# The end of a mixture of experts in a two-block network: expert 13's output two units earlier, a deeper weight stream, paired V groups, and another order of block 2's first steps

## The chip, the cores and the metric

The kernel runs on one core of a Trainium2 chip. The metric is the device time of one execution in microseconds (us), as the median of several runs. Before the change it is 2907.27 us, the median of three (2904.99 to 2908.48).

## The reference

The network works on 512 tokens of width 1024. Block 1 has two layers, each with one wide input product, differential attention, a gated convolution, attention to a memory, gates, an output product, a layer norm, and a mixture of 16 experts of which each token takes two, with a second layer norm. Block 2 begins with an RMS norm and one wide product, whose columns feed a recurrent branch (RWKV7), a state-space branch (S5) and gates; a convolutional feed-forward part ends it. Cut to what the change touches:

```python
for l in range(DEPTH):                       # block 1, two layers
    proj = x @ w_in[l]
    q, k, v, cb, cc, cu, qm, gates = jnp.split(proj, ...)
    ...
    x = layer_norm(DEEPNORM_ALPHA * x + mix, ln1_g[l], ln1_b[l])
    f = grouped_moe(x.reshape(B * S, D), w_router, router_bias,
                    w_exp_gate[l], w_exp_up[l], w_exp_down[l]).reshape(B, S, D)
    x = layer_norm(DEEPNORM_ALPHA * x + f, ln2_g[l], ln2_b[l])

def expert_block(args):                      # inside grouped_moe
    xblk, e = args
    h = jax.nn.silu(xblk @ w_gate[e]) * (xblk @ w_up[e])
    return h @ w_down[e]

h = rms_norm(x, norm_mix_pre[l])             # block 2
proj = h @ w_in[l]
gates = jax.nn.sigmoid(proj[..., N_RWKV_COLS + S5_WIDTH:] + b_gate[l])
```

## The kernel before, in words

Each product in 32-bit floats is made of three products of split numbers: high by high, high by low and low by high part. The weights come in units of 512 rows by 512 columns, 1.05 MB. A unit is loaded by SyncE's queue into a buffer (`wraw`, L100), ScalarE writes its high half (`whi`, L109) and VectorE its low half (`wlo`, L110), and TensorE makes 12 products of it for each tile of 128 tokens (L180). Raw units, halves and most other large tiles share one pool of 19 buffers. The program is written out in order: on every engine the instructions run in the order in which the Python emits them, and an engine whose next instruction waits runs nothing behind it.

`run_group` works through a group of units. At each unit it calls `ensure(split_to, load_to)`, which emits the splits up to `deep` units ahead of the current one and the loads `ahead` units further. Groups of order "t" go token tile by token tile, with a step `pre(t)` ahead of each; a group of order "h" goes over two halves of 256 tokens. `late` puts one of the three products of each step last. `tick()` advances side work such as the attention by one step.

`plan_moe` lists the experts: gate (two units, a and b), up (two), and one expert behind them the output product `down` (two units, x and y). I write g15a for a unit of expert 15's gate. The outputs of experts 0 to 13 go to a buffer in memory (`ye`, then `ybuf`); those of 14 and 15 stay on the chip as a high and a low half (`yh` on ScalarE, L1084, and `yl` on VectorE, L1085). The order at the end is

```
g14 u14 d13x d13y | last | g15a g15b u15a u15b d14x d14y d15x d15y | first group of the next stage
```

`last` sets `ahead, deep` to 1, 2 (in the mixture they are 7 and 3), calls `overflow`, which loads a count into a register and tests it in an If (L1147, L1149), and issues eight indirect transfers on GpSimd's queue (L1105). Each gathers 128 rows of `ybuf` and adds them to a tile of the residual, `xres`: two for each of the four token tiles.

`Combine` holds the steps behind the experts, each for one token tile: p (products that add experts 14 and 15 out of `yh` and `yl`, L1230), a (the sum on VectorE, L1237), s (statistics), b or c (the layer norm), and for block 2 r (the inverse root), h (the RMS norm, L1271), t (transposes, L335) and f (the low half of the transposed tile). They are listed in strings. In layer 1 the first group behind is half 0 of the V columns, in order "t", with one string for each tile. In block 2 it is `gate(0)`, in order "h": the first string serves tokens 0 to 255 and the second the rest. `rw_consts` writes constants of the recurrent branch and loads some, ahead of `gate(0)`.

Of the kernel before, what the change touches and what calls it, by code (L numbers as in the profile page):

```python
# [11 lines left out]
F32 = mybir.dt.float32  # L12
# [9 lines left out]
P = 128  # L22
D = 1024
T = 512
# [5 lines left out]
NE = 16  # L30
# [27 lines left out]
class Group:  # L58
# [7 lines left out]
    def __init__(self, units, tiles, operands, evac, free=512, before=None, order="k", pre=None,  # L66
                 lead=0, late=False):
        self.units, self.tiles, self.operands, self.evac, self.free, self.before = units, tiles, operands, evac, free, before
        self.order, self.pre, self.lead, self.last, self.late = order, pre, lead, False, late


@with_exitstack
def tile_kernel(ctx: ExitStack, tc: tile.TileContext, A, out):
# [87 lines left out]
    def run_group(g):  # L161
# [4 lines left out]

        def part(ui, t, cols=None):
            u = g.units[ui]
            if t not in psum:
                psum[t] = pb.tile([P, 512], F32, name="acc", tag="acc")  # L170
            trips = [g.operands(ui, kc, t, u) for kc in range(u.nk)]
            seq = [(kc, n) for kc in range(u.nk) for n in range(len(trips[kc]))]
            if g.late:
                seq.sort(key=lambda i: (i[1] == 2, i))
            for i, (kc, n) in enumerate(seq):
                l, r = trips[kc][n]
                if cols is not None:
                    r = r[:, cols]
                o = psum[t][:l.shape[-1], cols if cols is not None else slice(0, g.free)]
                nc.tensor.matmul(o, l, r, start=(ui == 0 and i == 0), stop=(ui == nu - 1 and i == len(seq) - 1))  # L180
                if state["fine"] and (kc, n) == (1, 2):
                    tick()

        if g.order == "k":
            for ui, u in enumerate(g.units):
                if g.last and ui == nu - 1:
                    ensure(i0 + nu, i0 + nu)
                else:
                    ensure(i0 + ui + state["deep"], i0 + ui + state["deep"] + state["ahead"],
                           step=STEP if g.tiles == 4 and state["deep"] == 2 else None)  # L190
                for t in range(g.tiles):
                    part(ui, t)
                    flush(1)
                    if ui == nu - 1:
                        g.evac(t, psum[t])
                    tick()
                u.raw = u.hi = u.lo = None
            return
        ensure(i0 + nu, i0 + nu + state["ahead"])
        halves = g.order == "h"  # L200
        n = 2 if halves else g.tiles
        for m in range(-g.lead, n):
            if g.pre and m + g.lead < n:
                g.pre(m + g.lead)
            if m < 0:
                continue
            if m == n - 1:
                ensure(i0 + nu + 1, i0 + nu + 1 + state["ahead"])
            for t in range(g.tiles) if halves else [m]:
# [6 lines left out]
                if m or not halves:  # L216
                    g.evac(t, psum[t])
        for u in g.units:
            u.raw = u.hi = u.lo = None
# [382 lines left out]
    def plan_block1(l):  # L602
# [6 lines left out]
        def cols(n):  # L609
            return column(w, l, ld, D, n)  # L610
# [9 lines left out]
        comb = Combine(0)  # L620

        def pre(t):
            if l == 0:
# [7 lines left out]
            if t == NT - 1:  # L631
                for n in ("x", "ln", "cm", "idx", "gs", "selT", "yh", "yl", "cnt", "dst", "orow"):
                    S.pop(n)
        pl.append(tok(cols(IN1["v"]), x, lambda t, p: ev_v(t, p, 0), before=mk((("v", 0), "vt")), order="t", pre=pre,
                      lead=1 - l, late=l > 0))

# [13 lines left out]
        for half in range(2):  # L650
            c = half * 512
            pl.append(tok(cols(IN1["q"] + c), x, rope_evac("q", half), before=mk((("q", half), "qT"))))
            pl.append(tok(cols(IN1["k"] + c), x, rope_evac("k", half), before=mk((("k", half), "kT"))))
            if half:
                pl.append(tok(cols(IN1["v"] + c), x, lambda t, p: ev_v(t, p, 1), before=mk((("v", half), "vt"))))
# [389 lines left out]
    def plan_moe(l):  # L1045
# [52 lines left out]
        def last():  # L1098

            finish(S.pop("route"))  # L1100
            state["ahead"], state["deep"] = 1, 2
            overflow(l)
# [6 lines left out]
        for e in range(NE):  # L1109
# [10 lines left out]
            def nxt(e=e):  # L1120
# [4 lines left out]
                if 0 < e <= NT:  # L1125
                    z = S["x"][(e - 1) // 2][:, (e - 1) % 2, :]
                    nc.scalar.activation(z, z, AF.Copy, scale=float(ALPHA))
                if e == NE - 2:
                    load_ln2(l)
# [3 lines left out]
            if e == 0:  # L1133
                S["moe0", l] = us[0]
            if e == NE - 1:
                pl.append(last)
            pl.append(one(us, lambda e=e: S["xeT"][e], ev_g, before=nxt))
            pl.append(one(eweight("w_exp_up", e, D, 512, 0), lambda e=e: S["xeT"][e], ev_u))
            if e:
                pl += down(e - 1)  # L1140
# [844 lines left out]
    def plan_block2():  # L1985
# [31 lines left out]
        def pre(m):  # L2017
            if m == 0:
                S["xT"] = new_feat("hT")
                S["pre"] = gain("norm_mix_pre_2")  # L2020
                comb.run("p0 p1 p2 p3 a0 s0 a1 b0 s1 r0 h0 t0 b1 f0 r1 a2 h1 t1 s2 f1 b2")
            else:
# [13 lines left out]
        def start0():  # L2036
            bv()

            def chain():
# [3 lines left out]
                yield from rwkv(1)  # L2043
            gens["r"] = spawn(chain())
        def gate(i):
            def ev(t, p):
# [3 lines left out]
                nc.gpsimd.dma_start(gdram[:, n, :], g)  # L2050
            return feat(cols(2304 + i * 512), x, ev, **(dict(order="h", pre=pre, before=rw_consts, late=True) if i == 0 else {}))

# [24 lines left out]

        pl.append(gate(0))
        pl.append(tok(cols(1792), x, ev_u, before=bu, sel=lambda t: slice(t, T, 4)))
        pl.append(start_s5)  # L2080
# [310 lines left out]
```

## Time and profile before

| | |
|---|---|
| median of three runs | 2907.27 us |
| profiled execution | 2902.47 us, its span 2900.5 us |
| mean granted clock of TensorE | 0.969 |
| TensorE busy | 2683.6 us (93%) |
| TensorE weight loads | 2164.9 us (75%) |
| VectorE, ScalarE busy | 1836.5 us (63%), 1314.9 us (45%) |
| GpSimd busy | 390.5 us (13%) |
| HBM over the span | 159 GB/s |

The times in the traces count from the start of the span. PE is TensorE, DVE VectorE, ACT ScalarE, POOL GpSimd and SP SyncE. In a timeline each row has the start, the duration and the instruction, and in brackets the idle time before it with what ended it. The mixture of layer 0 ends near 1050 us and that of layer 1 near 2010 us; these are the two places that the change touches.

### The profile page before, as it was taken

The page shows a single profiled execution, that of the slowest core. Times are in us where ns is not written, and L with a number is a line of the kernel's source. Part 1 is how long each engine was busy: PE and PEld are TensorE (multiplying, and loading weights), DVE is VectorE, ACT ScalarE, POOL GpSimd, SP SyncE. Part 2 cuts the span into 40 slices and gives each one's busy share as a digit, 9 for nine tenths or more (in the row PEclk, how much of TensorE's full clock was granted, in tenths as well). Part 3 has the DMA queues.
Part 4 walks back from the last instruction along what each step waited for, and adds up shares of the span by engine and source line. Part 5 has one row for each costly group of instructions (what it writes and reads, how often), then busy time and mean ns, then how long its engine had stood idle before and what let it go on. Part 6 is the DMA issues. An engine that isn't in the chain of part 4 may idle for free. (4 is left out here: it accounts for less than half of the span.)

```text
span 2900.5 us, 37504 instructions
## 1 busy us (share of the span) xinstructions
PE 2683.6 (93%) x14828; PEld 2164.9 (75%) x14828; DVE 1836.5 (63%) x2947; ACT 1314.9 (45%) x1935; POOL 390.5 (13%) x521
## 2 busy tenths in 40 slices
PE   8889999999899989999999979997978978999998
PEld 6677777887687768777788758875866756788887
DVE  4756555446799974565544579998478475655552
ACT  4334444332687743343533258875233542333441
POOL 2744200001100030000000110003221010000000
PEclk9999999999999999999999989998999989999999
DMA  5222413252999972112132489998321223323231
GB/s 192 88 81 84 166 44 98 92 174 93 370 402 409 366 216 73 59 59 73 59 102 102 148 307 391 409 377 253 124 95 59 70 77 132 117 93 102 73 131 44
DMA packets 223142, 464.25 MB, mean 160 GB/s; under 512 B 9849, under 2 KB 37681, under 8 KB 222448
## 3 DMA queue, kind: packets, MB, share of 16 engines
q1 hardware_dynamic: 194832, 359.69, 35.5%
q0 software_dynamic: 28128, 102.11, 10.0%
q8 instruction: 118, 1.93, 0.3%
q14 instruction: 64, 0.52, 0.1%
HBM read 419.29 MB, written 42.47 MB: 159 GB/s over the span
## 5 line engine op out<-in xcount | busy, mean ns | idle before, releaser
L110 DVE TENSOR_TENSOR wlo<-wraw,whi 128x1024 fp32r<-128x1024 f32 (+1 forms) x473 | 806.8, 1734 | 395.7 <-ACT whi L109 386.8
L109 ACT ACTIVATE whi<-wraw 128x1024 fp32r<-128x1024 f32 (+1 forms) x473 | 671.1, 1454 | 103.3 <-PE acc L180 38.5
L180 PE MATMUL acc<-whi,xeT 128*128 128x512 f32 x1024 | 329.5, 403 | 5.4 <-ACT whi L109 4.3
L180 PE MATMUL acc<-xTh,whi 128*128 128x512 f32 x640 | 257.5, 402 | 0.0
L180 PE MATMUL acc<-xTh,wlo 128*128 128x512 f32 x640 | 251.0, 392 | 1.6 <-DVE wlo L110 1.6
L180 PE MATMUL acc<-xTl,whi 128*128 128x512 f32 x640 | 250.2, 391 | 0.0
L180 PEld LDWEIGHTS acc<-whi,xeT 128*128 128x128 f32 x1024 | 190.8, 192 | 45.1 <-ACT whi L109 6.3
L180 PE MATMUL acc<-wlo,xeT 128*128 128x512 f32 x512 | 203.5, 398 | 6.8 <-DVE wlo L110 6.7
L180 PE MATMUL acc<-whi,xTh 128*128 128x512 f32 x384 | 163.1, 425 | 2.1 <-ACT xTh L338 2.1
L180 PE MATMUL acc<-whi,hT 128*128 128x512 f32 x512 | 162.5, 399 | 0.0
L180 PE MATMUL acc<-wlo,xTh 128*128 128x512 f32 x384 | 153.1, 399 | 0.0
L180 PE MATMUL acc<-whi,xTl 128*128 128x512 f32 x384 | 148.8, 398 | 1.7 <-DVE xTl L343 1.7
L475 ACT ACTIVATE pr<-sc,mx 128x128 f32<-128x128 f32 (+3 forms) x128 | 66.3, 523 | 182.8 <-DVE mx L473 168.4
L180 PE MATMUL acc<-h2Tl,whi 128*128 128x512 f32 (+1 forms) x384 | 144.1, 375 | 2.7 <-DVE h2Tl L343 2.7
L180 PE MATMUL acc<-h2Th,whi 128*128 128x512 f32 (+1 forms) x384 | 143.9, 375 | 2.3 <-ACT h2Th L338 2.3
L180 PE MATMUL acc<-h2Th,wlo 128*128 128x512 f32 (+1 forms) x384 | 143.7, 374 | 0.0
L180 PEld LDWEIGHTS acc<-xTh,wlo 128*128 128x128 f32 x640 | 120.5, 188 | 28.2 <-DVE wlo L110 2.0
L180 PEld LDWEIGHTS acc<-xTl,whi 128*128 128x128 f32 x640 | 120.9, 189 | 22.9
L180 PEld LDWEIGHTS acc<-xTh,whi 128*128 128x128 f32 x640 | 120.7, 189 | 23.0
L180 PEld LDWEIGHTS acc<-wlo,xeT 128*128 128x128 f32 x512 | 98.0, 191 | 31.8 <-DVE wlo L110 10.1
L278 POOL TENSOR_TENSOR ss<-ss,mhalf 128x1 f32<-128x1 f32 x64 | 35.2, 550 | 601.3 <-DVE ss L512 567.9
L180 PE MATMUL acc<-hTh,whi 128*128 128x512 f32 (+1 forms) x272 | 108.4, 405 | 0.2 <-ACT hTh L338 0.2
(689 smaller groups left out, 5619.2 us busy)
## 6 DMA issues: line engine op xcount, KB each, us to landing
wraw<-in_w_in SPq DMA_DIRECT2D x76, 1024.0 KB, 5.3
wraw<-in_w_exp_down SPq DMA_DIRECT2D x63, 1024.0 KB, 9.3
wraw<-in_w_exp_gate SPq DMA_DIRECT2D x62, 1024.0 KB, 8.9
wraw<-in_w_exp_up SPq DMA_DIRECT2D x60, 1024.0 KB, 11.6
wraw<-in_ffn_w_up SPq DMA_DIRECT2D x44, 512.0 KB, 4.6
ybuf<-ye POOLq DMA_DIRECT2D x28, 512.0 KB, 6.8
wraw<-in_w_out SPq DMA_DIRECT2D x12, 1024.0 KB, 5.1
wraw<-in_ffn_w_down SPq DMA_DIRECT2D x10, 1024.0 KB, 5.0
```

The lines of the kernel that those rows point to most:

```text
L109: nc.scalar.activation(u.hi[:, c], u.raw[:, c], AF.Copy)
L110: nc.vector.tensor_tensor(u.lo[:, c], u.raw[:, c], u.hi[:, c], op=ALU.subtract)
L180: nc.tensor.matmul(o, l, r, start=(ui == 0 and i == 0), stop=(ui == nu - 1 and i == len(seq) - 1))
L278: nc.gpsimd.tensor_tensor(o, x, mhalf.to_broadcast(list(x.shape)), op=ALU.pow)
L475: nc.scalar.activation(pr[:, c, :n], sc[c][:, :n], AF.Exp, bias=mx[:, c:c + 1], scale=0.125, accum_out=sm[:, c:c + 1])
```

## The change

The change has four parts.

- The order at the end of both mixtures. The output of expert 13 and `last` come two units earlier, ahead of expert 14's up product. The layer norm's weights are loaded one expert earlier.
- The weight stream. `last` sets `ahead, deep` to 2, 3 instead of 1, 2. The first group of the next stage sets them to 1, 2.
- Layer 1's V columns. The two halves are paired: a group may have a second one in `also`, whose products follow tile by tile. The later group of half 1 goes. The splits of the second half's two units are emitted behind the first `pre`.
- Block 2's start. The first string of steps has another order, another of the three products is put last in `gate(0)` (the one with the low half of the tokens instead of the one with the low half of the weights), and `rw_consts` moves from ahead of `gate(0)` to behind it.

```diff
--- before.py
+++ after.py
@@ -67,6 +67,7 @@
                  lead=0, late=False):
         self.units, self.tiles, self.operands, self.evac, self.free, self.before = units, tiles, operands, evac, free, before
         self.order, self.pre, self.lead, self.last, self.late = order, pre, lead, False, late
+        self.also = None
 
 
 @with_exitstack
@@ -164,14 +165,14 @@
         psum, nu = {}, len(g.units)
         i0 = units.index(g.units[0])
 
-        def part(ui, t, cols=None):
+        def part(ui, t, cols=None, g=g, psum=psum):
             u = g.units[ui]
             if t not in psum:
                 psum[t] = pb.tile([P, 512], F32, name="acc", tag="acc")
             trips = [g.operands(ui, kc, t, u) for kc in range(u.nk)]
             seq = [(kc, n) for kc in range(u.nk) for n in range(len(trips[kc]))]
             if g.late:
-                seq.sort(key=lambda i: (i[1] == 2, i))
+                seq.sort(key=lambda i: (i[1] == g.late, i))
             for i, (kc, n) in enumerate(seq):
                 l, r = trips[kc][n]
                 if cols is not None:
@@ -196,6 +197,7 @@
                     tick()
                 u.raw = u.hi = u.lo = None
             return
+        nall = nu + (len(g.also.units) if g.also else 0)
         ensure(i0 + nu, i0 + nu + state["ahead"])
         halves = g.order == "h"
         n = 2 if halves else g.tiles
@@ -204,8 +206,10 @@
                 g.pre(m + g.lead)
             if m < 0:
                 continue
+            if m == 0 and g.also:
+                ensure(i0 + nall, i0 + nall + state["ahead"])
             if m == n - 1:
-                ensure(i0 + nu + 1, i0 + nu + 1 + state["ahead"])
+                ensure(i0 + nall + 1, i0 + nall + 1 + state["ahead"])
             for t in range(g.tiles) if halves else [m]:
                 for ui in range(nu):
                     part(ui, t, slice(m * 256, m * 256 + 256) if halves else None)
@@ -215,7 +219,13 @@
                     tick()
                 if m or not halves:
                     g.evac(t, psum[t])
-        for u in g.units:
+                if g.also:
+                    p2 = {}
+                    for ui in range(len(g.also.units)):
+                        part(ui, t, None, g.also, p2)
+                        tick()
+                    g.also.evac(t, p2[t])
+        for u in g.units + (g.also.units if g.also else []):
             u.raw = u.hi = u.lo = None
 
     def run(plan):
@@ -619,6 +629,11 @@
             nc.scalar.activation(S["v", half][:, t, :], p, AF.Copy)
         comb = Combine(0)
 
+        def first_v():
+            state["ahead"], state["deep"] = 1, 2
+            for half in range(2):
+                S["v", half] = slot([P, 4, T], F32, "vt")
+
         def pre(t):
             if l == 0:
                 to_feat(S["x"][t // 2][:, t % 2, :], S["xT"], t)
@@ -631,8 +646,14 @@
             if t == NT - 1:
                 for n in ("x", "ln", "cm", "idx", "gs", "selT", "yh", "yl", "cnt", "dst", "orow"):
                     S.pop(n)
-        pl.append(tok(cols(IN1["v"]), x, lambda t, p: ev_v(t, p, 0), before=mk((("v", 0), "vt")), order="t", pre=pre,
-                      lead=1 - l, late=l > 0))
+        if l == 0:
+            pl.append(tok(cols(IN1["v"]), x, lambda t, p: ev_v(t, p, 0), before=mk((("v", 0), "vt")), order="t", pre=pre,
+                          lead=1))
+        else:
+            gs_ = [tok(cols(IN1["v"] + h * 512), x, lambda t, p, h=h: ev_v(t, p, h), order="t", pre=pre, late=2)
+                   for h in range(2)]
+            gs_[0].also, gs_[0].before = gs_[1], first_v
+            pl.append(gs_[0])
 
         def ev_qm(t, p):
             nc.scalar.activation(S["qm"][:, t, :], p, AF.Copy)
@@ -651,7 +672,7 @@
             c = half * 512
             pl.append(tok(cols(IN1["q"] + c), x, rope_evac("q", half), before=mk((("q", half), "qT"))))
             pl.append(tok(cols(IN1["k"] + c), x, rope_evac("k", half), before=mk((("k", half), "kT"))))
-            if half:
+            if half and l == 0:
                 pl.append(tok(cols(IN1["v"] + c), x, lambda t, p: ev_v(t, p, 1), before=mk((("v", half), "vt"))))
 
             def start(half=half):
@@ -1098,7 +1119,7 @@
         def last():
 
             finish(S.pop("route"))
-            state["ahead"], state["deep"] = 1, 2
+            state["ahead"], state["deep"] = 2, 3
             overflow(l)
             for j in range(2):
                 for t in range(NT):
@@ -1125,18 +1146,19 @@
                 if 0 < e <= NT:
                     z = S["x"][(e - 1) // 2][:, (e - 1) % 2, :]
                     nc.scalar.activation(z, z, AF.Copy, scale=float(ALPHA))
-                if e == NE - 2:
+                if e == NE - 3:
                     load_ln2(l)
                 if e + 1 < NE:
                     spawn(expert_in(l, e + 1))
             us = eweight("w_exp_gate", e, D, 512, 0)
             if e == 0:
                 S["moe0", l] = us[0]
-            if e == NE - 1:
+            pl.append(one(us, lambda e=e: S["xeT"][e], ev_g, before=nxt))
+            if e == NE - 2:
+                pl += down(e - 1)
                 pl.append(last)
-            pl.append(one(us, lambda e=e: S["xeT"][e], ev_g, before=nxt))
             pl.append(one(eweight("w_exp_up", e, D, 512, 0), lambda e=e: S["xeT"][e], ev_u))
-            if e:
+            if e and e != NE - 2:
                 pl += down(e - 1)
         pl += down(NE - 1)
         pl.append(drain)
@@ -2018,7 +2040,7 @@
             if m == 0:
                 S["xT"] = new_feat("hT")
                 S["pre"] = gain("norm_mix_pre_2")
-                comb.run("p0 p1 p2 p3 a0 s0 a1 b0 s1 r0 h0 t0 b1 f0 r1 a2 h1 t1 s2 f1 b2")
+                comb.run("p0 p1 p2 p3 a0 s0 a1 s1 b0 b1 r0 a2 r1 h0 t0 h1 t1 f0 f1 s2 b2")
             else:
                 comb.run("a3 r2 s3 h2 t2 b3 f2 r3 h3 t3 f3")
                 for n in ("x", "ln", "cm", "idx", "gs", "selT", "yh", "yl", "cnt", "dst", "orow", "pre"):
@@ -2042,13 +2064,16 @@
                     yield
                 yield from rwkv(1)
             gens["r"] = spawn(chain())
+        def first_g():
+            state["ahead"], state["deep"] = 1, 2
+
         def gate(i):
             def ev(t, p):
                 n = i * 4 + t
                 g = w2k([P, T], F32, "sgt")
                 nc.scalar.activation(g, p, AF.Sigmoid, bias=PV["b_gate_2"][:, n:n + 1])
                 nc.gpsimd.dma_start(gdram[:, n, :], g)
-            return feat(cols(2304 + i * 512), x, ev, **(dict(order="h", pre=pre, before=rw_consts, late=True) if i == 0 else {}))
+            return feat(cols(2304 + i * 512), x, ev, **(dict(order="h", pre=pre, before=first_g, late=1) if i == 0 else {}))
 
         def bu():
             S["s5u"] = slot([P, 16, 4, 32], F32, "s5u")
@@ -2076,6 +2101,7 @@
             s5_end()
 
         pl.append(gate(0))
+        pl.append(rw_consts)
         pl.append(tok(cols(1792), x, ev_u, before=bu, sel=lambda t: slice(t, T, 4)))
         pl.append(start_s5)
         pl.append(feat(cols(1536, 256), x, ev_wag, tiles=2, before=b0))
```

## Rows read from the trace of the kernel before

**Rows 1.** Windows: PE, PEld, DVE, ACT, POOL busy us; PEclk, DMA share, GB/s.

```profile
1014.00:1024.00 10.00, 9.61 (x44) 7.40 (x43) 8.70 (x6) 7.03 (x6) 0.54 (x1) 1.00 1.05 407
1028.00:1032.00 4.00, 2.41 (x11) 1.62 (x10) 3.93 (x2) 3.63 (x3) 3.60 (x1) 1.00 0.08 30
1038.00:1050.00 12.00, 9.28 (x38) 6.66 (x38) 8.86 (x6) 8.18 (x7) 8.41 (x4) 1.00 1.06 252
1061.91:1090.45 28.54, 26.61 (x122) 21.32 (x120) 20.93 (x30) 7.23 (x11) 3.55 (x7) 0.95 0.37 133
2050.00:2075.00 25.00, 25.00 (x144) 25.00 (x143) 5.86 (x5) 7.04 (x10) 5.49 (x11) 0.91 0.59 209
```

**Rows 2.** Waits of PE, 1950 to 2060: us in total, times, longest.

```profile
PE acc L180 <- DVE wlo L110: 3.2, 2, 1.6
```

**Rows 3.** Timeline of DVE, second end: start, us, instruction, idle before.

```profile
2003.32 0.74 DVE L1085 SCALAR_TENSOR_TENSOR yl<-acc,gs,yh 128x512 fp32r<-128x512 f32 x1
2004.22 0.86 DVE L1577 MEMSET rwc<- 128x960 f32 x1
...
2007.47 2.28 DVE L110 TENSOR_TENSOR wlo<-wraw,whi 128x2048 fp32r<-128x2048 f32 x1
2009.68 1.28 DVE L1237 TENSOR_TENSOR xres<-xres,yp 128x512 f32<-128x512 f32 x2
2010.87 1.28 DVE L352 BATCH_NORM_STATS2 lnst<-xres 128x6 f32<-128x512 f32 x2
...
2013.71 1.28 DVE L362 SCALAR_TENSOR_TENSOR xres<-xres,lnmv,lnp 128x1024 f32<-128x1024 f32 x1
...
2019.27 1.28 DVE L1271 SCALAR_TENSOR_TENSOR hpre<-xres,rms,gain 128x1024 f32<-128x1024 f32 x1 [1.21 <-POOL rms L278]
```

**Rows 4.** Timeline of PE, second end.

```profile
2027.04 1.94 PE L335 MATMUL tp<-ident,hpre 128*128 128x128 f32 x8 [4.46 <-DVE hpre L1271]
2028.82 0.58 PE L180 MATMUL acc<-hTh,whi 128*128 128x256 f32 x1
```

**Rows 5.** Timeline of POOL, second end, first and last of eight transfers.

```profile
1982.34 1.63 POOL L1105 DMA_INDIRECT xres<-ybuf,dst  x1 [6.30 <-DMA ybuf<-ye]
...
2000.91 1.55 POOL L1105 DMA_INDIRECT xres<-ybuf,dst  x1 [0.69 <-DMA xres<-ybuf,dst]
```

**Rows 6.** Tile view of xres, the last transfer alone (2000.91).

```profile
DMA to landing us min/median/max: 13.4/13.4/13.4
```

**Rows 7.** Timeline of POOL, first end, first and last of eight.

```profile
1028.29 3.60 POOL L1105 DMA_INDIRECT xres<-ybuf,dst  x1 [7.16 <-DMA ybuf<-ye]
...
1050.49 3.37 POOL L1105 DMA_INDIRECT xres<-ybuf,dst  x1 [0.56 <-DMA xres<-ybuf,dst]
```

**Rows 8.** Timeline of DVE, first end, a0.

```profile
1053.63 1.28 DVE L1237 TENSOR_TENSOR xres<-xres,yp 128x512 f32<-128x512 f32 x2 [1.18 <-DMA xres<-ybuf,dst]
```

**Rows 9.** Tile view of wraw: n0, n1, n2; n1 of the first end.

```profile
L100 SPq DMA_DIRECT2D wraw<-in_w_in x1: 554/554/554, 1970.1 to 1970.1; - x1
...
DMA to landing us min/median/max: 13.2/13.2/13.2
...
L100 SPq DMA_DIRECT2D wraw<-in_w_in x1: 383/383/383, 1987.9 to 1987.9; - x1
...
DMA to landing us min/median/max: 15.8/15.8/15.8
...
L100 SPq DMA_DIRECT2D wraw<-in_w_in x1: 368/368/368, 1990.8 to 1990.8; - x1
...
DMA to landing us min/median/max: 24.2/24.2/24.2
...
L100 SPq DMA_DIRECT2D wraw<-in_w_in x1: 377/377/377, 1033.0 to 1033.0; - x1
...
DMA to landing us min/median/max: 15.2/15.2/15.2
```

**Rows 10.** Timeline of ACT, second end, whi of n1.

```profile
2003.79 1.91 ACT L109 ACTIVATE whi<-wraw 128x2048 fp32r<-128x2048 f32 x1 [1.65 <-DMA wraw<-in_w_in]
```

## The prediction

> **What bounds the kernel now.** I read the share of each engine by stage first, then the waits of TensorE, then the engines' timelines around the two ends of the mixture of experts, then the loads there. Inside the mixture TensorE never stops and the DMA rings are full at 407 GB/s: 44 products in 10 us, so 0.227 us each, and a unit of 1.05 MB (12 products, 2.73 us of TensorE) needs 2.6 us of DMA [rows 1]. So nothing is to be had there. What can be had lies at the two stage ends, which I call the first (layer 0 into layer 1, near 1050 us) and the second (layer 1 into block 2, near 2010 us). There `last` puts eight indirect transfers on the queues, and the rings fall to 252 GB/s at a full busy share while they run [rows 1]. TensorE waits twice for a low half near each end, 3.2 us in all [rows 2]. After the last expert it stands still until VectorE has normalised the first token tiles: at the second end VectorE writes yl (2003.32), the constants of block 2 (2004.22 to 2007.47), the low half of unit n1 (2.28 us), and only then a0, at 2009.68; the first product of block 2 is at 2028.82 [rows 3, 4]. What precedes a0 on VectorE and ScalarE is therefore the path; I call the next stage's first four units n0 to n3.
>
> **The change, part by part.**
>
> **Order at the end.** Expert 13's output (`ye`) comes two units, 2 x 2.73 = 5.5 us, earlier, with the wait at the If behind it some 6 us. The indirect transfers start at 1982.34 and 2000.91 (first and last) and the last lands 13.4 us after its issue, at 2014.3 [rows 5, 6]; moved by 6 they end near 2008.3. At the first end they start at 1028.29 and 1050.49 [rows 7]; with the same 13.4 us the end goes from 1063.9 to 1057.9. That alone is a gain only where a0 waits for them: 1.18 us at the first end [rows 8], none at the second [rows 3].
>
> **What the loads lose by it.** The If makes SP wait until the loads that it has issued have landed: n0, issued at 1970.1, lands 13.2 us later at 1983.3, and the next load, n1, goes out only at 1987.9 [rows 9]. Before, the nine units ahead of d13y reach through d15y and n0. With u14 moved behind `last`, nine ahead reach only d15x. So d15y and n0 change sides: they are issued behind the If, as n1 is. d15x is two loads earlier in the stream, so it lands 2 x 2.6 earlier, at 1978.1, and d15y goes out then, n0 and n1 some 3 us apart behind it, as buffers are freed by the units of expert 15.
>
> Beside the indirect transfers loads crawl. n1 takes 15.8 us, n2 lands at 1990.8 + 24.2 = 2015.0, 11.3 us behind n1: 2.1 MB in 27.1 us, 77 GB/s, where 407 is the rate alone [rows 1, 9]. The first end agrees, 15.2 us for n1 [rows 9]. Three loads now stand where the first of the row stood. d15y: at best it passes before the indirect transfers have filled the rings (6 us, an estimate: twice the 2.6 us of the rate alone and a start), lands 1984; at worst as n1 did, 1993.9. n0 11.3 us behind: 1995.3 to 2005.2. n1 2006.6, or, as the indirect transfers are over at 2008.3 and the rest goes at full rate, 2010.2. I take the middle, 2008.4. At the first end everything stands 954.05 us earlier (1982.34 against 1028.29), so d15y goes out near 1024. There the rings stood nearly empty, share 0.08, for 4 us around the first transfer [rows 1], which favours the near bound: n1 at 1024 + 5 + 2 x 11.3 = 1051.6 at best, 1058.8 at worst; I take 1052.5.
>
> **Depth 2, 3.** With `deep` 3 the splits of n0 and n1 stand in program order before the evictions of d15x and d15y: whi n1 before yh15 on ScalarE, wlo n1 before yl15 on VectorE. Before, n1's split came after them. So behind the wait for n1 are queued yh15, yl15, the products p0 to p3 on TensorE, and a0. From n1's landing to a0: whi 1.91 [rows 10], wlo 2.28, yl 0.74 [rows 3], the last products of p0 and the steps between, 0.6 by estimate: 5.6 us (5.53 in rows). a0 then comes at 2014.0 (2012.2 to 2015.8) against 2009.68: +4.3 (+2.5 to +6.1). At the first end 1058.1 (1057.2 to 1064.4) against 1053.63 [rows 8]: +4.5 (+3.6 to +10.8). The waits for low halves (3.2 us at each end) do go, since splits are a unit further ahead, but the time goes into the wait for n1: nothing.
>
> **The steps of block 2 and its constants.** From a0 to the first product is 19.14 us now [rows 3, 4]. In the new string h0 no longer stands alone behind its square and the root on GpSimd (the 1.21 us wait, [rows 3]): a0 s0 a1 s1 take 2 x (1.19 + 1.65) by the starts in the rows, b0 and b1 2 x 2.56, a2 and the small steps 1.5, h0 1.25; that is 13.5, then h1 1.25 beside the transposes of t0; t1's transposes from 15.8, and 1.78 from them to the first product [rows 4]: 17.6, so -1.5. Everything of the first half's other products hides behind TensorE at half clock as before. The constants (3.25 us on VectorE and their transfers on GpSimd) stood before a0; they move behind the gate group, where VectorE is busy 5.9 of 25 us [rows 1], so cost nothing; without that cover 3.25. Their removal pays only if a0 is not waiting for n1. It is, so nothing. Second end: 4.3 - 1.5 = +2.8 (+1.0 to +4.6).
>
> **Paired V in layer 1.** The V group takes 28.54 us [rows 1] for 96 products of 0.227, 21.8. Of the 6.7 left, the clock (0.95 of full on average) is 1.4 and the transposes of three tiles at 0.97 (half of 1.94, which is at half clock) 2.9; at most 2.4 is waiting for VectorE, and with twice the products per tile that wait is covered. The second half's 21.8 us leave their later place unchanged. 0 to -2.4; I take -1.8, since 10.9 us of products per tile exceed the 7.1 (28.54 / 4) at which the group now goes from tile to tile. The units n2 and n3 must be split before; they land when the indirect transfers end, near 1058 to 1062, and TensorE reaches them only a tile later, so the cover is some 6 us; beyond it each us late is a us. First end: 4.5 - 1.8 = +2.7 (+1.2 to +10.8).
>
> **The sum.** +2.8 + 2.7 = +5.5 us on the profiled execution, 2902.47, makes 2908; that execution is 4.8 below the median of the runs, 2907.27, to which the forecast belongs: 2912.8, rounded 2913. Bounds of the mechanism, +2 to +15. What measurement tells from no change is 0.2%, 5.8 us, so the forecast lies right at that edge.
>
> **A rule against the split of the rings.** In the rows a load gets 77 of about 250 GB/s, under a third [rows 1, 9]. The Trainium skill, DMA: Bandwidth & Descriptors, "Queues, rings and completion order", says that a DMA engine goes round the queue rows it has work for, one packet each. If the packets of both rings were alike, each would get half; the trace of before does not agree with half, but shows no moment with three loads queued.
>
> **The rivals.**
> 1. Equal shares: both rings move the same bytes while both have work. Half of 250 is 125 GB/s, 8.4 us a unit: n1 at 1978.1 + 25.2 = 2003.3, a0 2008.9 (-0.8), with the new steps -2.3; first end 1049.2, a0 1054.8 (+1.2), with V -0.6. With d15y through early, 3.4 less at each: -3 to -10, say -6.5, 2901. For it: the early rings are not full [rows 1]. Against: 15.8 and 24.2 [rows 9].
> 2. Loads in time. If the loads behind the If run as those of the mixture do, a0 follows TensorE: without 3.2 of waits and with no constants and no n1 before yl beyond its split, a0 at the second end comes near 2000, -9.6, with the steps -11; at the first end a0 is held by the indirect transfers, 6 earlier, -6.1, with V -8. -19, 2888. For it: the rows' 1.65 us wait of ScalarE shows n1 only just late now [rows 10]. Against: the same rows at 77 GB/s.
> 3. Slower: the first load behind the If takes what n1 took, 15.2 and 15.8 us, at both ends, and the next follow at 11.3. Then a0 is at the far bounds: +6.1 and +10.8, with the gains of 1.5 and 1.8 +13.6, 2921. It decides once n1 lands later than about 2010 and 1054. For it: the row itself [rows 9]. Against: the empty rings at 1028 to 1032.
>
> **How the numbers follow.** Forecast (+2 to +9): 0.50, of it 0.27 within 0.2% and 0.23 above. Equal shares 0.20, half of it faster, half within. In time 0.17, faster. Slower rival 0.13. Together faster 0.27, same 0.37, slower 0.36. The range 2890 to 2923 leaves out most of the in-time case and the tail above the slow one, some 0.18; the forecast's own range is 2909 to 2917.
>
> **What would show it.** Right: d15y, n0 and n1 issued after the If and landing near 1990, 2000 and 2008; ScalarE idle on the load of n1 just before yh15; a0 at 2012 to 2016 and 1057 to 1060 with the waits for low halves gone; from a0 to the first gate product 17.6 us; the constants after 2050; a shorter gap between the tiles of V. Wrong: n1 landing before 2003, or a0 held by xres; d15y issued ahead of the If; VectorE late with the halves of n2 and n3 between V's tiles; or the second attention of layer 1 waiting, since its V products no longer cover the first one's steps.

## The result, and the profile after

The changed kernel takes 2923.92 us (median of five runs, 2922.01 to 2928.45) against 2906.42 for the kernel before (five runs): ratio 1.0062, 95% interval 1.0048 to 1.0076. It is 17.5 us slower, 1 us beyond the far end of the predicted range, 2890 to 2923. Of the cases written down the slower rival, 2921, lies nearest.

The profiled execution took 2928.45 us, 4.5 above the median of its kernel; the one of before was 4 below. The two traces therefore differ by 26 us where the medians differ by 17.5. The head of the page:

```profile
span 2926.9 us, 37478 instructions
## 1 busy us (share of the span) xinstructions
PE 2698.5 (92%) x14828; PEld 2176.4 (74%) x14828; DVE 1838.1 (63%) x2945; ACT 1317.9 (45%) x1935; POOL 395.6 (14%) x521
```

The work of the engines is the same to about 1%; what is longer is the time in which TensorE waits, or runs at a lower clock. To see where, the first start of some tiles, from the tile views of each trace, is compared with the trace of before. Each number is the difference of the two starts in us (the last four rows belong to the experiments' end), so a step from one column to the next is what the stage between cost or gave:

```
                   first   p0,     first    last K   first   last     p0,      a0,      first    end of
                   expert  first   V        evicted  expert  gate/up  second   second   product  span
                   layer 0 end     product  layer 1  layer 1 product  end      end      block 2
before (us)         730.5  1046.4  1061.9   1256.3   1695.6  1987.3   2001.3   2009.7   2028.8   2900.5
changed              -1.2    +0.5    +9.8    +28.0    +17.6   +16.7    +14.5    +24.0    +23.9    +26.4
without pairing      +1.2    -0.3    +8.8     +7.6     +7.4    +5.6     +3.4    +14.0    +13.9    +14.5
pairing alone        +2.7    +3.3    +2.9    +22.8    +14.1   +14.1    +14.1    +14.3    +14.8    +17.5
order alone          -0.7    +0.4    +4.5     +3.4     +3.2    +3.2     +7.4    +13.8    +13.8    +16.8
depth alone          +0.4    -3.0    +0.7     +1.5     +2.7    +0.6     -1.5     -1.1     +3.1     +5.9
constants alone      -0.3    -1.3    -1.1     -0.8     -0.6    -0.6     -0.6     -3.2     -3.1     -0.5
steps alone          +0.5    -0.5    -0.4     -0.5     -0.4    -0.4     -0.4     -0.4     -1.5     -4.0
made from the parts  -1.8    -1.3    +1.1     +1.6     +2.5    +2.3     +2.3     -3.4     -2.4     -1.4
pairing, gate group  +0.3    -1.2    -1.4    +18.7     +3.9    +3.9     +3.8     +3.9     +3.9     +6.9
```

In the changed kernel 9.3 us go between p0 and the first V product, 9.5 between p0 and a0 at the second end, and layer 1 loses too. The K column is an eviction, and in the kernel before 22 of the 96 products of V's second half run ahead of it; so I count layer 1 by the first product of each group instead. The V group takes 48.1 us for 192 products where it took 28.8 for 96; with 21.8 for the 96 that were moved there it saves 2.5. The stretch from the second half's K group to the memory branch's second gate group takes 275.4 us where it took 286.0, only 10.6 less, though the 21.8 left it: 11.2 us lost.

At the second end the loads of d15y, n0 and n1, in the tile view of the changed kernel:

```profile
L101 SPq DMA_DIRECT2D wraw<-in_w_exp_down x1: 383/383/383, 1997.8 to 1997.8; - x1
...
DMA to landing us min/median/max: 5.8/5.8/5.8
...
L101 SPq DMA_DIRECT2D wraw<-in_w_in x1: 367/367/367, 2001.2 to 2001.2; - x1
...
DMA to landing us min/median/max: 15.5/15.5/15.5
...
L101 SPq DMA_DIRECT2D wraw<-in_w_in x1: 367/367/367, 2004.0 to 2004.0; - x1
...
DMA to landing us min/median/max: 24.8/24.8/24.8
```

Set against [rows 9]: n1 took 15.8 us before and takes 24.8 now, landing at 2028.8. The timelines of ScalarE, then VectorE, behind it:

```profile
2018.56 0.67 ACT L1105 ACTIVATE yh<-acc,gs 128x512 fp32r<-128x512 f32 x1
2028.89 1.91 ACT L110 ACTIVATE whi<-wraw 128x2048 fp32r<-128x2048 f32 x1 [9.66 <-DMA wraw<-in_w_in]
2030.70 0.67 ACT L1105 ACTIVATE yh<-acc,gs 128x512 fp32r<-128x512 f32 x1
```

```profile
2030.83 2.29 DVE L111 TENSOR_TENSOR wlo<-wraw,whi 128x2048 fp32r<-128x2048 f32 x1 [9.19 <-ACT whi L110]
2033.04 0.75 DVE L1106 SCALAR_TENSOR_TENSOR yl<-acc,gs,yh 128x512 fp32r<-128x512 f32 x1
2033.70 0.68 DVE L1259 TENSOR_TENSOR xres<-xres,yp 128x512 f32<-128x512 f32 x1
```

ScalarE stands 9.66 us until n1 has landed, and only then writes the last yh; VectorE stands as long, then writes n1's low half, yl and a0. From landing to a0 it is 4.9 us (5.6 predicted). TensorE's waits there show the same queue from the other side, p0 waiting for yh where [rows 2] had waits for low halves:

```profile
PE yp L1252 <- ACT yh L1105: 10.9, 2, 8.1
PE tp L345 <- DVE hpre L1293: 5.7, 1, 5.7
PE yp L1252 <- DVE yl L1106: 3.2, 2, 1.6
```

### The profile page after: what moved, and what is told of

The parts are those of the page before. It is cut to its first block, busy times and chain, and to the rows that moved or that the text cites. A ratio compares the mean times of both kernels' runs of the same rounds, so it can differ in the third digit from the quotient of the medians.

```text
span 2926.9 us, 37478 instructions
## 1 busy us (share of the span) xinstructions
PE 2698.5 (92%) x14828; PEld 2176.4 (74%) x14828; DVE 1838.1 (63%) x2945; ACT 1317.9 (45%) x1935; POOL 395.6 (14%) x521
## 5 line engine op out<-in xcount | busy, mean ns | idle before, releaser
L111 DVE TENSOR_TENSOR wlo<-wraw,whi 128x1024 fp32r<-128x1024 f32 (+2 forms) x471 | 807.1, 1742 | 405.7 <-ACT whi L110 396.8
L110 ACT ACTIVATE whi<-wraw 128x1024 fp32r<-128x1024 f32 (+2 forms) x471 | 670.6, 1459 | 126.8 <-PE acc L181 30.3
```

The costliest lines, as they stand in the source:

```text
L110: nc.scalar.activation(u.hi[:, c], u.raw[:, c], AF.Copy)
L111: nc.vector.tensor_tensor(u.lo[:, c], u.raw[:, c], u.hi[:, c], op=ALU.subtract)
```

## The experiments

Each kernel was timed against the kernel before on the same chip, in five rounds. "Alone" means the kernel before with that part only.

**Without the pairing.** The V groups of layer 1 as before, all else as changed:

```diff
-            gs_[0].also, gs_[0].before = gs_[1], first_v
-            pl.append(gs_[0])
+        pl.append(tok(cols(IN1["v"]), x, lambda t, p: ev_v(t, p, 0), before=first_v, order="t", pre=pre,
+                      lead=1 - l, late=2 * l))
...
-            if half and l == 0:
+            if half:
```

> The changed kernel without the pairing: V's second half is back in its place after the second half's K group; order, depth and block 2 stay as changed. In the trace of the changed kernel layer 1 lost some 10 us between the last K group and its mixture, and the pairing saved 2.5 us at the V group itself. Theory A (the removed V group was the cover under which the attention's steps of layer 1 ran, its loss costs 8 to 10): 5 to 8 us faster than the changed kernel, 2916 to 2919, and no loss between the K group and the mixture. Rival (the cover was not needed, the loss in layer 1 is a slower clock of that one execution): 2 to 3 us slower than the changed kernel, 2926.

2917.32 us, ratio 1.0040 (1.0026 to 1.0053): 6.6 faster than the changed kernel's median. In the table the loss between the K group and the mixture is gone (+7.6 to +7.4), and the stretch of layer 1 takes 285.8 us. Theory A holds.

**The pairing alone.**

```diff
+            gs_[0].also, gs_[0].before = gs_[1], first_v
...
-            if half:
+            if half and l == 0:
```

> The kernel before with the pairing alone (order, depth 1, 2, steps of block 2 as before). Theory A: 5 to 8 us slower than before, 2912 to 2915. Rival (pairing pays, as forecast): 0 to 2.4 us faster, 2904 to 2907.

2916.62 us, ratio 1.0034 (1.0022 to 1.0046): 11.2 us slower against a median of 2905.41, more than the 5 to 8 expected. The V group itself gives 0.8 (49.8 us for 192 products, 28.8 before for 96, with 21.8 moved), and the stretch behind it costs 11.8 (276.0 us where 286.0 less 21.8 was due). So the step "their later place unchanged" fails with nothing else changed.

**The order alone.** Expert 13's output and `last` two units earlier, depth 1, 2:

```diff
+            pl.append(one(us, lambda e=e: S["xeT"][e], ev_g, before=nxt))
+            if e == NE - 2:
+                pl += down(e - 1)
+                pl.append(last)
```

> The kernel before with the order at the end alone: expert 13's output and the step with the If and the indirect transfers two units earlier; depth 1, 2, no pairing, block 2 as before. Theory B (the loads of d15y, n0 and n1 fall behind the indirect transfers): n1 lands 4 to 8 us later than before at both ends and a0 with it, 8 to 14 us slower, 2915 to 2921. Rival (the depth 2, 3 alone does it, by the splits that stand before the evictions): within 3 us of before.

2920.78 us, ratio 1.0052 (1.0037 to 1.0066): 15.4 slower, a little over what was expected. Its d15y and n0 at the second end (tile view):

```profile
L101 SPq DMA_DIRECT2D wraw<-in_w_exp_down x1: 383/383/383, 1985.8 to 1985.8; - x1
...
DMA to landing us min/median/max: 15.0/15.0/15.0
...
L101 SPq DMA_DIRECT2D wraw<-in_w_in x1: 367/367/367, 1988.5 to 1988.5; - x1
...
DMA to landing us min/median/max: 24.4/24.4/24.4
```

n0 lands 12.1 us behind d15y (2012.9 against 2000.8), 87 GB/s of the 256 that move in that time. Nothing but the order is needed for the loss.

**The depth alone.** The old order, depth 2, 3:

```diff
-            state["ahead"], state["deep"] = 1, 2
+            state["ahead"], state["deep"] = 2, 3
```

> The kernel before with depth 2, 3 across the stage end alone, set back in the next stage's first group; old order, no pairing, block 2 as before. Theory B: the loads go out as before, n1 lands as before; the waits for low halves go, but yl stands behind n1's low half: between 0 and +2 us. Rival (the depth does the harm): 6 us slower or more. Second rival (the waits for low halves, 3.2 us at each end, were on the path): 4 to 6 us faster, 2901.

2906.01 us, ratio 0.9999 (0.9990 to 1.0007): no change. p0 comes 3 us earlier at the first end, since the waits for low halves are gone, and the first V product does not: it goes into the next wait, as predicted.

**Early output, the If in its old place.** Expert 13's output early, `last` ahead of expert 15's gate:

```diff
+            if e == NE - 1:
+                pl.append(last)
             pl.append(one(us, lambda e=e: S["xeT"][e], ev_g, before=nxt))
             if e == NE - 2:
                 pl += down(e - 1)
-                pl.append(last)
```

> The kernel before with expert 13's output two units earlier, but the step with the If and the indirect transfers left in its old place ahead of expert 15's gate; depth 1, 2, no pairing, block 2 as before. Theory B1 (the harm comes from the two loads, d15y and n0, that changed to the far side of the If): they are ahead of the If again, the indirect transfers start some 5 us earlier than before as their data has landed, n1 lands as before; within -4 to +1 us of before, 2901 to 2906. Rival B2 (the harm comes from the indirect transfers that start earlier and so meet more of the loads): 8 us slower or more.

2906.91 us, ratio 0.9997 (0.9988 to 1.0006). d15y and n0 are ahead of the If again, n1 takes 13.8 us at the second end, and the 15 us are gone, though the transfers at the first end start 6.6 us earlier than before (1021.7 against 1028.3). B1 holds, B2 falls. Starting the transfers earlier gives nothing by itself either.

**The transfers held back.** The order alone, but GpSimd copies one column of expert 15's hidden product before it issues the transfers:

```diff
+                if e == NE - 1:
+                    hold = work.tile([P, 1], F32, name="hold", bufs=1)
+                    nc.gpsimd.tensor_copy(hold, h[:, 0:1])
+                    transfers()
```

> The order alone, as in the run of that name, but the eight indirect transfers wait on GpSimd for expert 15's hidden product (one small copy of its first column is added as the wait). The If stays early, so d15y, n0 and n1 are still issued behind it. Theory B (the loads are slow because they share the rings with the indirect transfers): d15y, n0 and n1 land within 5 to 8 us of their issue, a0 is then held by the indirect transfers at some 2 us later than before; 2 to 7 us slower than before, 2907 to 2912, and 8 to 13 faster than the order alone. Rival (the loads are late because the If issues them late): as slow as the order alone, 2921.

2915.46 us, ratio 1.0031 (1.0020 to 1.0042): 8.9 slower than its kernel before, where the order alone was 15.4 slower than its own. That is 6.5 less, and 8 to 13 were expected. But the loads tell the theories apart. d15y and the third load behind it, n2, at the second end, with the transfers at 1996.16 and later (tile view, then GpSimd's timeline):

```profile
L101 SPq DMA_DIRECT2D wraw<-in_w_exp_down x1: 382/382/382, 1987.6 to 1987.6; - x1
...
DMA to landing us min/median/max: 4.9/4.9/4.9
...
L101 SPq DMA_DIRECT2D wraw<-in_w_in x1: 368/368/368, 1996.0 to 1996.0; - x1
...
DMA to landing us min/median/max: 5.9/5.9/5.9
```

```profile
1993.82 2.18 POOL L1136 COPY hold<-eg 128x1 f32<-128x1 f32 x1 [18.60 <-DVE eg L1132]
1996.16 1.64 POOL L1121 DMA_INDIRECT xres<-ybuf,dst  x1 [0.16 <-issue]
```

Still issued behind the If, d15y lands in 4.9 us instead of 15.0, and n0, n1 and n2 in 5.3 to 5.9. It is the sharing of the rings that makes the loads late, not their late issue. The loss that is left lies at the same two ends, where the transfers themselves are now late; it was not taken apart further.

**Block 2's part alone.** The new string, the other product last, the constants behind the gate group:

```diff
-                comb.run("p0 p1 p2 p3 a0 s0 a1 b0 s1 r0 h0 t0 b1 f0 r1 a2 h1 t1 s2 f1 b2")
+                comb.run("p0 p1 p2 p3 a0 s0 a1 s1 b0 b1 r0 a2 r1 h0 t0 h1 t1 f0 f1 s2 b2")
...
+        pl.append(rw_consts)
```

> The kernel before with block 2's part alone: the other order of the first steps, the other product last, the constants behind the gate group. The prediction's step: 1.5 us from a0 to the first product, and, as n1 lands at its old time, up to 1.7 us of the constants' 3.25: 1.5 to 3.2 us faster, 2902 to 2904. Rival (from the trace of the changed kernel, where a0 to the first product took 18.9 us and not 17.6: the new string gives nothing): the constants alone, 0 to 1.7 us faster.

2898.82 us, ratio 0.9973 (0.9963 to 0.9982): 7.7 us faster, more than twice the expected. This is the fastest kernel here, beside the steps alone.

**Its two halves.** The constants alone, and the steps with the other product last alone:

```diff
-            return feat(..., **(dict(order="h", pre=pre, before=rw_consts, late=True) if i == 0 else {}))
+            return feat(..., **(dict(order="h", pre=pre, before=first_g, late=2) if i == 0 else {}))
...
+        pl.append(rw_consts)
```

> The kernel before with block 2's constants moved behind the gate group, nothing else. Block 2's part alone was 7.7 us faster than before. Theory C (the constants stood before a0 and are the greater half): 2 to 4 us faster, 2903 to 2905. Rival (the constants are hidden, the steps do it): within 1 us of before.

2901.66 us, ratio 0.9984 (0.9975 to 0.9992): 4.0 us faster. In its trace a0 is 2.6 nearer to p0 than before, since no constants stand ahead of it.

```diff
+                comb.run("p0 p1 p2 p3 a0 s0 a1 s1 b0 b1 r0 a2 r1 h0 t0 h1 t1 f0 f1 s2 b2")
...
+            return feat(..., **(dict(order="h", pre=pre, before=first_g, late=1) if i == 0 else {}))
```

> The kernel before with block 2's other order of steps and the other product last, the constants ahead of the gate group as before. Theory C: the rest of the 7.7 us, 3 to 5 us faster, 2902 to 2904, and in the trace the first product earlier after a0. Rival (the constants do it): within 1 us of before.

2898.85 us, ratio 0.9980 (0.9970 to 0.9989): 6.8 us faster by the medians, 5.8 by the ratio. The windows around the first gate products, first of the constants alone (old string), then of the steps alone:

```profile
2025.70:2027.70 2.00, 1.85 (x8) 1.56 (x8) 1.84 (x3) 0.60 (x1) 0.35 (x1) 0.50 0.00 0
2027.70:2029.70 2.00, 2.00 (x11) 2.00 (x11) 1.90 (x3) 0.00 (x0) 0.00 (x0) 0.50 0.00 0
2029.70:2031.70 2.00, 2.00 (x18) 2.00 (x17) 1.93 (x6) 1.15 (x2) 0.94 (x2) 0.91 0.27 113
```

```profile
2024.00:2026.00 2.00, 1.44 (x8) 1.04 (x7) 1.73 (x3) 1.19 (x2) 0.00 (x0) 0.50 0.04 8
2026.00:2028.00 2.00, 1.76 (x12) 1.38 (x12) 1.02 (x3) 1.09 (x2) 0.00 (x0) 0.87 0.00 0
2028.00:2030.00 2.00, 2.00 (x19) 2.00 (x18) 1.97 (x4) 0.00 (x0) 0.00 (x0) 1.00 0.00 0
```

PEclk is the third number from the right. With the old string the transposes of t0 and t1 stand 6.4 us apart, TensorE is idle between them, and the first products run at half clock for 4.4 us (3.8 to 4.8 in the seven traces of experiments with this string; 1.7 in the trace of before). With the new string the two stand 2.5 us apart, the products follow directly, and the clock is back at full when they start. That is so in the steps alone and in block 2's part alone. It is not so in the three other traces with this string and the same 2.5 us: the products start at half clock for 2.3 us in the last experiment below, for 2.4 without the pairing and for 4.2 in the changed kernel. So the distance alone does not decide it. The string and the other product last were not run apart.

**A version made from the parts.** Early output with the If in place, block 2's part, and n1's low half written behind h1:

```diff
-                comb.run("... h0 t0 h1 t1 f0 f1 s2 b2")
+                comb.run("... h0 t0 h1 t1 w0 f0 f1 s2 b2")
...
+            def low():
+                nc.vector.tensor_tensor(u.lo, u.raw, u.hi, op=ALU.subtract)
```

> A version made from the parts: expert 13's output early with the If in its old place, depth 1, 2, no pairing, block 2's new steps with the constants behind, and n1's low half in block 2 written behind the step h1 instead of ahead of a0. If a0 at the second end stands behind VectorE's work for n1 and the constants, it comes 4 to 5 us earlier; with 0 to 4 from the indirect transfers at the first end 4 to 8 us faster than before, 2897 to 2901. Rival (n1's low half is only moved into the chain from a0 to the first product): 0 to 2 us faster.

2900.22 us, ratio 0.9980 (0.9971 to 0.9989). Faster than before, but not than block 2's part alone. a0 does come 5.7 us nearer to p0 (+2.3 to -3.4 against before), and 1.0 is given back until the first product, which runs at half clock again; the profiled trace ends only 3.7 nearer to its p0.

**The pairing with another light group in V's place.** The pairing alone, with the first gate group of layer 1's convolution branch ahead of the convolution's second group:

```diff
+            r = feat(cols(IN1["gate"] + i * D + g * 512), x, ev_g, before=before)
+            if between:
+                pl.append(r)
+                between()
```

> The kernel before with the pairing alone, and in layer 1 the first gate group of the convolution's branch moved ahead of the convolution's second group (it is as light as the V group that went: one copy on ScalarE for each tile). So the attention's steps meet the convolution's evictions where they did before. Theory A1 (the loss of the pairing comes from heavy attention steps that meet the convolution's evictions): 0 to 3 us faster than before, 2904 to 2907, 9 or more faster than the pairing alone. Rival A2 (eight steps of cover are gone in any order, and the attention ends later): as slow as the pairing alone, 9 to 12 slower than before.

2910.48 us, ratio 1.0022 (1.0012 to 1.0031): 4.8 slower than before by the medians. Of the 11.8 us that the stretch behind V lost, 6.3 are left (it takes 270.5 us). Over the convolution's groups and this gate group A1 holds: TensorE is idle there for 2.5 us, where it was 6.0 in the pairing alone and 3.1 before, and the clock stays full. What is left lies at its two sides. At the end of the K group TensorE waits 3.4 us as in the pairing alone, with 1.7 lost to the clock. Behind the convolution it is idle for 4.2 us against 0.5 before, since the attention's tail runs there: its last output is evicted at 1506.6, against 1480.8 before and 1516.3 in the pairing alone. That is what A2 says. So A1 explains about half, and A2 much of the rest; idle time and clock make 5.5 of the 6.3.

> The same with block 2's part as well, which alone was 7.7 us faster. If A1 holds, 8 to 10 us faster than before, 2897 to 2899, and the fastest version here; by A2 2 to 4 us slower than before.

With block 2's part as well 2904.66 us, ratio 0.9993 (0.9984 to 1.0002): no change that can be told, and behind block 2's part alone. Both expectations miss. The parts alone would add to -2.9 (-7.7 + 4.8), and 1.0 was measured; the trace shows a term that does not add. From the first product of block 2 to the end of the span it is 2.4 us longer than in block 2's part alone, and its first products run at half clock (the first window):

```profile
2030.50:2032.50 2.00, 2.00 (x10) 1.97 (x10) 1.83 (x3) 0.60 (x1) 0.00 (x0) 0.50 0.00 0
```

## Why the prediction was wrong

**The step that failed: "the second half's 21.8 us leave their later place unchanged".** It was set at nothing; alone the pairing costs 11.2 us. The prediction has the loss among its signs of being wrong, attention that waits since V no longer covers it, but no term, rival or price for it. The windows of the stretch from the second half's K group to the memory branch's second gate group, of the kernel before and then of the pairing alone:

```profile
1213.30:1499.30 286.00, 276.49 (x1371) 212.97 (x1369) 160.33 (x401) 129.90 (x326) 16.98 (x31) 1.00 0.22 70
1237.30:1513.30 276.00, 260.99 (x1273) 199.30 (x1271) 155.74 (x397) 126.53 (x318) 16.98 (x31) 0.98 0.20 63
```

TensorE is idle for 15.0 us in place of 9.5, and at half clock for 13.6 us in place of none, which costs 6.8. The two make 12.3 us, for the 11.8 lost. What V's second half had covered was not counted: in its place TensorE worked through 76 instructions of the attention between V's products, and V loads the other engines with one copy a tile. Without it some of these steps follow each other with no product between, some meet the convolution's evictions, and the attention ends later. TensorE's longest waits in the stretch, before and then in the pairing alone:

```profile
PE po L506 <- ACT pr L475: 2.5, 3, 1.2
PE sc L463 <- ACT ya L523: 1.9, 4, 1.1
```

```profile
PE po L516 <- ACT pr L485: 5.2, 3, 3.4
PE sc L473 <- ACT ya L533: 3.9, 4, 1.7
PE po L516 <- ACT aT L508: 1.8, 2, 1.3
PE po L532 <- DVE osb L526: 1.3, 1, 1.3
```

And the clock in the same stretch (windows of the pairing alone):

```profile
1275.00:1277.00 2.00, 0.01 (x1) 0.01 (x1) 1.03 (x3) 0.84 (x3) 0.00 (x0) 0.90 0.46 177
...
1279.10:1283.10 4.00, 4.00 (x15) 2.97 (x14) 2.19 (x9) 1.96 (x7) 0.55 (x1) 0.50 0.02 4
1349.10:1351.10 2.00, 0.72 (x7) 0.73 (x7) 1.18 (x3) 1.88 (x3) 0.00 (x0) 1.00 0.00 0
1351.10:1355.10 4.00, 4.00 (x13) 3.14 (x13) 3.92 (x7) 1.54 (x5) 0.00 (x0) 0.57 0.00 0
1489.10:1491.10 2.00, 0.25 (x2) 0.23 (x2) 1.09 (x1) 1.99 (x6) 0.00 (x0) 1.00 0.00 0
1491.10:1495.10 4.00, 4.00 (x11) 2.42 (x11) 3.06 (x10) 0.74 (x2) 0.55 (x1) 0.57 0.86 262
```

Three times TensorE falls to half clock behind a stretch in which it was mostly idle (busy for 0.01, 0.72 and 0.25 of 2 us): for 6.8, 3.4 and 3.4 us.

**Mis-sized: the V group.** 1.8 us were taken from it, of at most 2.4 of waiting. Its idle time falls from 1.9 to 0.9 us, alone and in the changed kernel. With the clock of each trace it gives 0.8 alone, 2.5 in the changed kernel, and 1.2 there against the run without the pairing.

**Mis-sized: the loads.** Mechanism right, at both ends, in the run with the order alone; the size was 8.8 without the gains and measured 15.4, inside the bounds of 6.1 to 16.9 but not near the middle that I took. Two terms are off. d15y was to go out at 1978.1 and 1024, when d15x has landed. In the order alone it goes out at 1985.8 and 1028.5, 4.5 and 5.2 us later by that trace's own position (+3.2 and -0.7). d15x had landed 5 us before (1980.9). What SP then waits for, 4.4 us, is VectorE's write of a low half, behind which a raw buffer comes free; I had counted it as free. The waits of SP, 1980 to 1996:

```profile
SPq L101 <- DVE wlo L111: 6.7, 2, 4.4
```

And d15y at the second end then took 15.0 us, the far bound, not the middle. The transfers also ended later than the 6 us earlier that I set: at the second end 2013.0 in the order alone, 4.5 earlier than before by its position. In the changed kernel d15y took 5.8 us, the near bound, but n0 and n1 land 13.1 and 12.1 apart, where 11.3 was taken, and the transfers end at 2029.3, only 1.7 earlier by position. So a0 at the second end is 7.3 later by the position of the mixture's last product (24.0 - 16.7), where 4.3 was taken and 6.1 was the bound. At the first end it is 9.8 later by the position of the first expert, where 4.5 was taken and 10.8 was the bound.

**Right: the depth.** The waits for low halves go and the time goes into the next wait: no change alone. In the changed kernel p0 waits for yh, 10.9 us in all, as predicted; but without the depth the same n1 holds a0 on VectorE, and from the mixture's last gate or up product to block 2's first product the order alone loses 10.6 and the kernel without the pairing 8.3.

**Mis-sized: block 2.** The steps give 5.8 to 6.8 us alone, where 1.5 was the term. From a0 to the first product they gave 1.1 of that; "at half clock as before" was wrong there, as the clock is back when the first products start. Behind the first product the trace of the steps alone is 2.5 us shorter than that of before, and 4.8 to 5.6 shorter than those of the seven experiments with the old string. In the changed kernel the clock does not come back: from a0 to the first product it is 0.2 us shorter than before, and those products run at half clock until 2056.9. The constants give 4.0 alone, and the prediction had them at nothing only because a0 would wait for n1; that held.

**The rivals.** Equal shares falls, and in time with it: with three loads queued n0 still needs 12.1 us, where equal shares had 8.4. The queues in these 12.1 us of the order alone, 2000.8 to 2012.9:

```profile
q0 software_dynamic: 562, 1.97, 77.5%
q1 hardware_dynamic: 568, 1.13, 27.9%
```

q1, the loads, has packets of 2.0 KB, and q0, the transfers, of 3.5: as many packets, but 36% of the bytes. The Trainium skill, DMA: Bandwidth & Descriptors, "Queues, rings and completion order", has a DMA engine take a packet from each queue row in turn; by that rule, the trace agrees, the counts come out equal, 562 and 568, and not the bytes. Whether the packets that the trace counts are those of the page is not shown here. The slower rival was near at the two ends (6.1 and 10.8 us, for 7.3 and 9.8 in the changed kernel), though by a slow first load that the second end did not have, and it had no loss in layer 1. That its 2921 lies nearest is in part luck.

The sum of the parts alone is +11.2 for the pairing, +15.4, +0.6 and -7.7, 19.5 us, and the whole is +17.5. That they come so near is luck too: in the changed kernel the pairing costs 6.6 and not 11.2, and the order, the depth and block 2's part together 11.9 and not 8.3.

## What to carry to other kernels

A group that is moved away takes its cover with it: before an edit counts it as work that only changes place, list which side work runs under it, and which evictions that work will meet instead. A step at which a queue waits (here an If) splits the stream of loads; what counts is how many loads stand on its far side, and what shares the rings there. To bring two short bursts of TensorE together just ahead of a long group can be worth more than the time between them, if the trace shows the group starting at half clock; but it need not be, as two of the five traces here had that gain and three did not.

## What was not expected of the hardware

The clock's part, and how little of it is fixed by the order of the work. With the transposes of two tiles 2.5 us apart in place of 6.4 the following products started at full clock in two traces of five and at half clock in three, and where they started at full the gain was some 5 us against the other traces with the old string (2.5 against that of before) beside the 1.1 of the steps themselves. In layer 1 of the pairing alone, gaps in TensorE's work (the longest wait is 3.4 us) were followed by half clock for 3.4 to 6.8 us, three times in one stretch, where the kernel before ran at full clock throughout. But a gap is not always followed so. Behind V's second half the kernel before and block 2's part alone run the same instructions, with TensorE busy for 2.41 and 2.36 of 4.2 us, and only the second falls to half clock (windows of before, then of block 2's part alone):

```profile
1279.00:1283.20 4.20, 2.41 (x15) 1.19 (x13) 2.46 (x7) 1.66 (x5) 0.00 (x0) 1.00 0.70 207
1283.20:1286.60 3.40, 3.24 (x18) 2.53 (x19) 1.39 (x7) 1.46 (x6) 0.55 (x1) 1.00 0.14 55
```

```profile
1279.00:1283.20 4.20, 2.36 (x15) 1.18 (x14) 2.34 (x6) 1.78 (x5) 0.00 (x0) 1.00 0.69 218
1283.20:1286.60 3.40, 3.40 (x13) 2.56 (x14) 1.51 (x7) 1.35 (x6) 0.55 (x1) 0.51 0.11 42
```

The same fall is in four more traces without the pairing, 1.7 us each, and not in four others. So of a single trace's clock loss a microsecond or two can belong to that execution.
